# The block norms' reciprocal root in eight VectorE operations, and the weights' subtractions kept out of it

## The chip, the cores and the metric

One core of a Trainium2 chip runs the whole program in one launch. Its engines are TensorE (PE; PEld is its weight load), VectorE (DVE), ScalarE (ACT), GpSimd (POOL) and SyncE (SP), which here issues the transfers. The metric is the device time of one execution in microseconds, the median over runs.

## The reference, cut to what matters

Two blocks of depth 2 are chained over one sequence of S = 256 tokens of width D = 1024, in fp32, with FFNs of width 2816. The first block has per layer an FFN, a mixer (a gated delta net and a latent attention) and a second FFN. The second block begins with an FFN on the tokens `x` and on a context `ctx`, has a state-space mixer, two FFNs, a pool mixer and an FFN. A final norm ends it. Each of these parts is of one shape:

```python
h = x * rsqrt(mean(x * x, -1) + EPS)      # the block norm
h = h * (1 + scale) + shift               # scale, shift, gate: from the conditioning, by ada_w
x = x + gate * part(h)
```

## The kernel before, in words

The tokens lie in two tiles of 128 partitions (NT = 2), each in two halves of 512 columns. Every product with a weight is done in three matmuls with rounded parts of both operands: a weight's hi and lo part and the tokens' hi and lo part. L351 multiplies the tokens' lo with the weight's hi, L352 hi with hi, and L353 the tokens' hi with the weight's lo; only L353 needs the weight's lo.

A weight comes in units of 128x1024. `load_unit` issues the load into one of six raw buffers on SP's queue, rounds it to hi on ScalarE (L345, or L339 in halves of 512) and subtracts hi from it on VectorE (L346, or L340) to get lo. hi and lo have five buffers of their own; units loaded far ahead ("deep") use general pages `pg` and the half-size lines. Three lanes keep the order of the units: `in_order("dma" | "hi" | "lo", ins)` ties each instruction to the one that `last[kind]` holds, an order on one engine that is fixed when the program is built. All else on an engine is ordered by the scheduler, at build time too, by the program's order among what it takes to be ready.

A norm is made by `Prep`. `Prep.a(t)` squares the two halves of token tile t on ScalarE with a sum (L683), adds the two sums (L684), calls `rsqrt` (L214 to L229: L218 scales and adds EPS, L219 and L220 make the first guess out of the bits, then three steps of L223 and L227) and multiplies both halves (`scaled`, L690). The ten operations from L684 to the last L227 work on one element per partition and each needs the one before. `Prep.b(t)` then transposes on TensorE (L248), modulates while evicting (L702 on VectorE, L700 on ScalarE) and splits the result into hi (L723) and lo (L724), in `hTa` or `hTb`, which the next product reads. The pool mixer's `PoolPrep` replaces `scaled` by a product with a second tensor, `sc` (L1927), and has no `b`; its product L1947 reads the scaled rows.

At the end of a part, `ending.done(t)` multiplies with the gate (L784), adds to the stream (L785) and calls `a(t)` of the next part's norm at once, `b(t)` some units later. There, at a seam, the last eight units of a part hold the second token tile's matmuls back; while TensorE does those, the first eight units of the next part are loaded and split, and tile 0's norm is made. The context's norms, `p0` and `p1`, are made in the middle of an FFN's down-projection: `a(0)` after its fourth unit and `a(1)` after its fifth; `p1` reads its rows back out of DRAM, where the context's first FFN wrote them (L2040 writes, L2025 reads).

There are 14 such norms of two token tiles each. The very first is made while `m.first` is set (the conditioning of the first part is still being computed).

Of the kernel before, what the change touches and what calls it, by code (L numbers as in the profile page):

```python
# [12 lines left out]
I32 = mybir.dt.int32  # L13
AF = mybir.ActivationFunctionType
ALU = mybir.AluOpType
# [4 lines left out]
D = 1024  # L20
# [4 lines left out]
EPS = 1e-6  # L25
# [50 lines left out]
def block_kernel(ctx, tc, A, out):  # L76
    nc = tc.nc
    V, G, T = nc.vector, nc.gpsimd, nc.tensor
# [27 lines left out]
    def nm(s):  # L106
        names[0] += 1
        return f"{s}_{names[0]}"
# [7 lines left out]
    def pg(dt=F32):  # L116
        return pgp.tile([P, 512], dt, tag="pg", name=nm("pg"))

    def small(n, dt=F32, tag="sm", bufs=None):
        return smp.tile([P, n], dt, tag=f"{tag}{n}", name=nm(tag), **({"bufs": bufs} if bufs else {}))  # L120
# [8 lines left out]
    def C(n):  # L129
        a, w = CI[n]  # L130
        return con[:, a:a + w]
# [7 lines left out]
    def rows_load(srcs):  # L139

        st = pg()
        at = 0
        for a in srcs:
            load(st[at:at + a.shape[0], 0:P], a)
            at += a.shape[0]
        return st, at
# [28 lines left out]
    def vectors():  # L175

        if adab:
            return
        st = pg()
        at = 0  # L180
        for a in (r128(A["c"][0]), r128(A["c_2"][0]), r128(A["c_ctx_2"]), rr(A["norm_ffn1"]), rr(A["norm_mix"]),
                  rr(A["norm_ffn2"]), A["norm_g_2"].rearrange("l n (k p) -> (l n k) p", p=P)):
            load(st[at:at + a.shape[0], 0:P], a)
            at += a.shape[0]
            yield
        l_vecs = st, at
        l_first = l_adab(*first_key)
        yield
        vecs = rows_put("vecs", l_vecs)
        for b in (0, 1, 2):  # L190
            if b != first_key[0]:
                ACT.activation(cond[:, 8 * b:8 * b + 8], vecs[:, 8 * b:8 * b + 8], AF.Silu)
        gain.update({(0, l, s): vecs[:, 24 + 16 * s + 8 * l: 32 + 16 * s + 8 * l] for l in range(2) for s in range(3)})
        gain.update({(1, l, s): vecs[:, 72 + 24 * l + 8 * s: 80 + 24 * l + 8 * s] for l in range(2) for s in range(3)})
        adab[first_key] = rows_put("adab0", l_first)
# [12 lines left out]
    def bcm(ap, n):  # L208

        return ap.unsqueeze(1).to_broadcast([P, n, ap.shape[1]])  # L210
# [3 lines left out]
    def rsqrt(out_, in_, scale, eps, n):  # L214

        v, y, t = small(n, tag="rx"), small(n, tag="ry"), small(n, tag="rt")
        i = small(n, I32, tag="ri")
        V.tensor_scalar(out=v, in0=in_, scalar1=-0.5 * scale, scalar2=-0.5 * eps, op0=ALU.mult, op1=ALU.add)  # L218
        V.tensor_scalar(out=i, in0=v.bitcast(I32), scalar1=1, scalar2=None, op0=ALU.logical_shift_right)  # L219
        V.tensor_scalar(out=y.bitcast(I32), in0=i, scalar1=-1, scalar2=0x5F3759DF - 0x400000 + 0x40000000, op0=ALU.mult, op1=ALU.add)  # L220
        for k in range(3):
            if n == 1:
                V.scalar_tensor_tensor(out=t, in0=y, scalar=v, in1=y, op0=ALU.mult, op1=ALU.mult)  # L223
            else:
                V.tensor_mul(t, y, y)
                V.tensor_mul(t, t, v)
            V.scalar_tensor_tensor(out=(out_ if k == 2 else y), in0=t, scalar=1.5, in1=y, op0=ALU.add, op1=ALU.mult)  # L227
# [73 lines left out]
    last = {}  # L301
# [366 lines left out]
    class Prep:  # L668
# [9 lines left out]
        def a(self, t):  # L678
            ss, r = small(2, tag="ss"), small(1, tag="rstd")
            xh = [self.xs(t, h) for h in range(2)]  # L680
            for h in range(2):
                xn = self.xn[t, h] = pg()
                ACT.activation(xn, xh[h], AF.Square, accum_out=ss[:, h:h + 1])  # L683
            V.tensor_add(ss[:, 0:1], ss[:, 0:1], ss[:, 1:2])  # L684
            rsqrt(r, ss[:, 0:1], 1.0 / D, EPS, 1)
            for h in range(2):
                self.scaled(t, h, xh[h], r)

        def scaled(self, t, h, src, r):
            V.tensor_scalar(out=self.xn[t, h], in0=src, scalar1=r, scalar2=None, op0=ALU.mult)  # L690

        def feat(self, t, h):
            q = ps()
# [1202 lines left out]
    class PoolPrep(Prep):  # L1896
        def early(self):

            for _ in range(4):
                yield  # L1900
            self.q, self.w = [], []
            self.sums, self.bias = pg(), pg()
            for h in range(2):
                load(self.sums[32 * h:32 * h + 1, :].rearrange("p (g l) -> p g l", l=S), A["poolc"][2 * h:2 * h + 2, :].unsqueeze(0))
                load(self.bias[32 * h:32 * h + 1, :], A["pool_b_2"][0, 2 * h:2 * h + 2, :].rearrange("g d -> (g d)").unsqueeze(0))
            for g in range(4):
                self.w.append(pg())
                load(self.w[g].rearrange("p (k d) -> p k d", k=2), A["pool_w_2"][0, g].rearrange("(k p) d -> p k d", p=P))
            yield
            for h in range(2):  # L1910
                psc = pg()
                load(psc, A["pool_scale_2"][0, h * 512:(h + 1) * 512].partition_broadcast(P))
                yield
                V.tensor_mul(psc, psc, self.m.has("gate", 0)[:, h * 512:(h + 1) * 512])
                V.tensor_mul(self.bias[32 * h:32 * h + 1, :], self.bias[32 * h:32 * h + 1, :], psc[32 * h:32 * h + 1, :])
                yield
                for g in (2 * h, 2 * h + 1):
                    w_ = self.w[g].rearrange("p (k d) -> p k d", k=2)
                    V.tensor_mul(w_, w_, bcm(psc[:, g % 2 * S:g % 2 * S + S], 2))
                    yield  # L1920
            for g in range(4):
                self.q.append(pg())
                load(self.q[g].rearrange("p (t l) -> p t l", t=NT), A["poolq"][g].rearrange("(t p) l -> p t l", p=P))
            yield
# [249 lines left out]
```

## Time and profile before

| | us |
|---|---|
| median of 3 runs | 3010.07 |
| least and most of the 3 | 3007.27 and 3012.36 |
| the profiled execution, its own time | 3013.99 |
| its span in the trace | 3012.2 |
| TensorE busy | 2908.4 (97%) |
| VectorE busy | 2190.8 (73%) |
| ScalarE busy | 1356.9 (45%) |

The trace is that of one execution. Its mean granted clock of TensorE is 0.984 of full speed. Busy time counts the instructions of an engine, not its waits. In a timeline row, the brackets at the end tell how long the engine stood idle before the instruction, and what released it.

### The profile page before, as it was taken

Reading aid. Unit: us, or ns where it says so; the run is one execution under the profiler, and the core shown is the slowest. Engines: PE = TensorE matmul, PEld = TensorE weight load, DVE = VectorE, ACT = ScalarE, POOL = GpSimd, SP = SyncE. Lnnn points to the kernel's source line nnn. Section 1 sums busy time; section 2 is a strip of 40 time slices with the busy share of each in tenths; the row PEclk is TensorE's granted clock in tenths of the full one; section 3 lists DMA queues with packets and bytes.
Section 4 is the critical chain, followed back from the end, with each engine's and each line's share of the span. In section 5 each row is a group of like instructions: output and inputs, shape, how many; then the busy total and the mean of one; then the engine's idle time right before and its main releaser. Section 6 shows DMA issues by size and latency. Waiting matters only on the chain.

```text
span 3012.2 us, 42589 instructions
## 1 busy us (share of the span) xinstructions
PE 2908.4 (97%) x16059; PEld 2432.2 (81%) x16059; DVE 2190.8 (73%) x4002; ACT 1356.9 (45%) x2123; POOL 105.5 (4%) x100
## 2 busy tenths in 40 slices
PE   7999999999999999999999999999899999999998
PEld 4988776779889788767798888888776798897797
DVE  6778757777687875677987664786788875887654
ACT  4555323554454443245546222455546544543443
POOL 1000110000000002000000000000022000000000
PEclk9999999999999999999999999999999999999999
DMA  8875534468778842244676455764434586788464
GB/s 269 293 271 190 175 103 117 130 191 265 254 242 275 298 138 79 72 137 152 219 242 212 153 175 160 263 216 140 158 98 133 189 278 242 228 289 297 155 188 133
DMA packets 275496, 589.04 MB, mean 196 GB/s; under 512 B 28731, under 2 KB 72905, under 8 KB 275291
## 3 DMA queue, kind: packets, MB, share of 16 engines
q1 hardware_dynamic: 275291, 586.32, 59.6%
q8 instruction: 126, 2.06, 0.3%
q14 instruction: 79, 0.65, 0.1%
HBM read 582.05 MB, written 4.19 MB: 195 GB/s over the span
## 4 chain that ended last, share of the span: by engine, by line
PE 72%; DVE 16%; DMA 6%; ACT 3%; issue 3%; SPq 0%; DVEq 0%; ACTq 0%
PE mm L351 18%; PE mm L352 17%; PE mm L353 17%; PE mm L411 5%; PE mm L384 4%; DVE lo L346 3%; DMA ad<-ada_w 3%; PE ps L248 3%; DVE acc L540 2%; PE ps L1260 1%; ACT hi L345 1%; PE ps L1267 1%; PE ps L558 1%; DMA raw<-ffn_w_down 1%; DVE pg L1611 1%
## 5 line engine op out<-in xcount | busy, mean ns | idle before, releaser
L345 ACT CAST hi<-raw 128x1024 fp32r<-128x1024 f32 x587 | 613.9, 1048 | 876.5 <-PE mm L352 349.7
L346 DVE TENSOR_TENSOR lo<-raw,hi 128x1024 fp32r<-128x1024 f32 x587 | 710.9, 1219 | 304.9 <-ACT hi L345 295.1
L351 PE MATMUL mm<-hTa,lo 128*128 128x256 f32 (+1 forms) x2160 | 650.8, 302 | 17.6 <-DVE lo L346 9.6
L352 PE MATMUL mm<-hTa,hi 128*128 128x256 f32 (+1 forms) x2160 | 643.7, 298 | 0.0
L353 PE MATMUL mm<-hTa,hi 128*128 128x256 f32 x1872 | 531.6, 284 | 0.0
L351 PEld LDWEIGHTS mm<-hTa,lo 128*128 128x128 f32 x2160 | 414.1, 192 | 34.4 <-DVE lo L346 10.5
L352 PEld LDWEIGHTS mm<-hTa,hi 128*128 128x128 f32 x2160 | 414.4, 192 | 13.4 <-issue 1.4
L540 DVE SCALAR_TENSOR_TENSOR acc<-ad,cond,acc 128x1024 f32<-128x1024 f32 x238 | 308.3, 1295 | 88.8 <-DMA ad<-ada_w 86.6
L353 PEld LDWEIGHTS mm<-hTa,hi 128*128 128x128 f32 x1872 | 360.1, 192 | 0.0
L351 PE MATMUL mm<-hi,pg 128*128 128x512 f32 x828 | 329.5, 398 | 1.6 <-DVE pg L844 0.9
L353 PE MATMUL mm<-lo,pg 128*128 128x512 f32 x828 | 324.1, 392 | 2.7 <-DVE lo L346 2.5
L352 PE MATMUL mm<-hi,pg 128*128 128x512 f32 x828 | 323.6, 391 | 0.0
L351 PE MATMUL mm<-hi,hTa 128*128 128x512 f32 (+1 forms) x444 | 182.8, 412 | 23.0 <-DVE hTa L724 11.7
L411 PE MATMUL mm<-hTb,raw 128*128 128x256 f32 x896 | 205.0, 382 | 0.0
L411 PEld LDWEIGHTS mm<-hTb,raw 128*128 128x128 f32 x896 | 169.0, 191 | 29.5 <-issue 7.9
L351 PEld LDWEIGHTS mm<-hi,pg 128*128 128x128 f32 x828 | 156.0, 188 | 36.2 <-issue 2.2
L353 PEld LDWEIGHTS mm<-lo,pg 128*128 128x128 f32 x828 | 155.7, 188 | 36.4 <-DVE lo L346 4.2
L353 PE MATMUL mm<-lo,hTa 128*128 128x512 f32 (+1 forms) x468 | 184.1, 394 | 0.0
L352 PE MATMUL mm<-hi,hTa 128*128 128x512 f32 (+1 forms) x468 | 183.9, 393 | 0.0
L352 PEld LDWEIGHTS mm<-hi,pg 128*128 128x128 f32 x828 | 156.0, 188 | 32.9 <-issue 2.2
L384 PE MATMUL mm<-raw,hTb 128*128 128x512 f32 x320 | 151.0, 603 | 0.0
L340 DVE TENSOR_TENSOR pg<-raw,pg 128x512 fp32r<-128x512 f32 x202 | 128.8, 683 | 4.9 <-ACT pg L339 3.4
(461 smaller groups left out, 4407.7 us busy)
## 6 DMA issues: line engine op xcount, KB each, us to landing
ad<-ada_w SPq DMA_DIRECT2D x272, 512.0 KB
raw<-ffn_w SPq DMA_DIRECT2D x264, 512.0 KB
raw<-ffn_w_down SPq DMA_DIRECT2D x110, 512.0 KB
raw<-w_in SPq DMA_DIRECT2D x104, 512.0 KB
raw<-ffn_w_gate SPq DMA_DIRECT2D x88, 512.0 KB
raw<-ffn_w_up SPq DMA_DIRECT2D x88, 512.0 KB
raw<-ssd_w_in SPq DMA_DIRECT2D x60, 512.0 KB
raw<-w_branch_a SPq DMA_DIRECT2D x16, 512.0 KB
```

Source lines behind the costliest of these rows:

```text
L248: T.transpose(o[:, sl], src[:, sl], ident)
L340: in_order(lane, eng.tensor_sub(lo[j], r, hi[j]))
L345: in_order("hi", ACT.copy(hi[:, 0:m], raw[:, 0:m]))
L346: in_order(lane, eng.tensor_sub(lo[:, 0:m], raw[:, 0:m], hi[:, 0:m]))
L351: T.matmul(o, sl, mh, start=first, stop=False)
L352: T.matmul(o, sh, mh, start=False, stop=False)
L353: T.matmul(o, sh, ml, start=False, stop=last)
L384: T.matmul(d[c0 // 512][:, 0:min(cw, c0 + 512) - c0], sf, wt[c0 // 512], start=k == 0, stop=k == kt - 1)
L411: T.matmul(acc[m][:, 0:S], wt[0][:, SL[m]], hT.whole[:, k, :], start=k == 0, stop=k == KD - 1)
L540: after_edge(V.scalar_tensor_tensor(out=o, in0=w, scalar=sc, in1=o, op0=ALU.mult, op1=ALU.add))
L558: T.matmul(q, ones, self.acc[i][h], start=True, stop=True)
L1260: T.matmul(blk(y[:, H2[h]]), M[t][:, sl], odd(Ub[t][:, sl]), start=True, stop=True)
```

## The change

`Prep.a` no longer adds the two sums and calls `rsqrt`. One operation with a pointer scalar makes s = ss0 + ss1 + D·EPS; one integer operation makes the first guess out of the bits of s, with the opposite sign and off by a constant factor; three steps of two operations each follow. What the steps leave out, the factor -sqrt(2D), goes into `scaled` as a second multiplication in the same instruction, and for the pool mixer into its tensor `sc`, by one more operation for each half in `early`. These are eight chained operations on one element per partition in place of ten. The last of them is put into `last["lo"]`, other than in the first norm: every weight's subtraction that comes later in the program must stand behind it on VectorE. The norm itself is not tied to the subtractions before it.

```diff
--- before.py
+++ after.py
@@ -681,13 +681,21 @@
             for h in range(2):
                 xn = self.xn[t, h] = pg()
                 ACT.activation(xn, xh[h], AF.Square, accum_out=ss[:, h:h + 1])
-            V.tensor_add(ss[:, 0:1], ss[:, 0:1], ss[:, 1:2])
-            rsqrt(r, ss[:, 0:1], 1.0 / D, EPS, 1)
+
+            s, z, u = small(1, tag="rx"), small(1, tag="ry"), small(1, tag="rt")
+            V.tensor_scalar(out=s, in0=ss[:, 0:1], scalar1=ss[:, 1:2], scalar2=D * EPS, op0=ALU.add, op1=ALU.add)
+            V.tensor_scalar(out=z.bitcast(I32), in0=s.bitcast(I32), scalar1=-0.5, scalar2=0x5F3759DF - 0x400000, op0=ALU.mult, op1=ALU.add)
+            for k in range(3):
+                V.scalar_tensor_tensor(out=u, in0=z, scalar=s, in1=z, op0=ALU.mult, op1=ALU.mult)
+                ins = V.scalar_tensor_tensor(out=(r if k == 2 else z), in0=u, scalar=-1.5, in1=z, op0=ALU.add, op1=ALU.mult)
+
+            if last.get("lo") is not None and self.m.first is None:
+                last["lo"] = ins.ins
             for h in range(2):
                 self.scaled(t, h, xh[h], r)
 
         def scaled(self, t, h, src, r):
-            V.tensor_scalar(out=self.xn[t, h], in0=src, scalar1=r, scalar2=None, op0=ALU.mult)
+            V.tensor_scalar(out=self.xn[t, h], in0=src, scalar1=r, scalar2=-(2.0 * D) ** 0.5, op0=ALU.mult, op1=ALU.mult)
 
         def feat(self, t, h):
             q = ps()
@@ -1912,6 +1920,7 @@
                 load(psc, A["pool_scale_2"][0, h * 512:(h + 1) * 512].partition_broadcast(P))
                 yield
                 V.tensor_mul(psc, psc, self.m.has("gate", 0)[:, h * 512:(h + 1) * 512])
+                V.tensor_scalar(out=self.m.has("sc", 0)[h], in0=self.m.has("sc", 0)[h], scalar1=-(2.0 * D) ** 0.5, scalar2=None, op0=ALU.mult)
                 V.tensor_mul(self.bias[32 * h:32 * h + 1, :], self.bias[32 * h:32 * h + 1, :], psc[32 * h:32 * h + 1, :])
                 yield
                 for g in (2 * h, 2 * h + 1):
```

## Rows read from the trace of the kernel before

**Rows 1.** Profile page: busy time by engine, shares of the last chain

```profile
PE 2908.4 (97%) x16059; PEld 2432.2 (81%) x16059; DVE 2190.8 (73%) x4002; ACT 1356.9 (45%) x2123; POOL 105.5 (4%) x100
PE 72%; DVE 16%; DMA 6%; ACT 3%; issue 3%; SPq 0%; DVEq 0%; ACTq 0%
```

**Rows 2.** Waits of TensorE: line, waited for, us in total, times, longest us

```profile
PE mm L351 <- DVE hTa L724: 11.7, 9, 3.3
PE mm L351 <- DVE lo L346: 9.6, 7, 5.2
PE ps L1729 <- ACT pg L1616: 6.6, 1, 6.6
PE ps L248 <- DVE pg L690: 2.4, 6, 1.2
PE ps L1947 <- DVE pg L1927: 1.9, 1, 1.9
```

**Rows 3.** Timeline of VectorE, an undisturbed norm: start us, us, operation

```profile
2785.53 0.15 DVE L684 TENSOR_TENSOR ss<-ss 128x1 f32<-128x1 f32 x1
...
2785.72 0.15 DVE L218 TENSOR_SCALAR rx<-ss 128x1 f32<-128x1 f32 x1
...
2786.28 0.22 DVE L223 SCALAR_TENSOR_TENSOR rt<-ry,rx 128x1 f32<-128x1 f32 x1
2786.54 0.16 DVE L227 SCALAR_TENSOR_TENSOR ry<-rt,ry 128x1 f32<-128x1 f32 x1
2786.73 0.22 DVE L223 SCALAR_TENSOR_TENSOR rt<-ry,rx 128x1 f32<-128x1 f32 x1
...
2787.63 1.41 DVE L1927 SCALAR_TENSOR_TENSOR pg<-xres,rstd,pg 128x512 f32<-128x512 f32 x2
```

**Rows 4.** Timeline of VectorE, seam from the FFN to layer 1's mixer

```profile
1039.30 0.14 DVE L684 TENSOR_TENSOR ss<-ss 128x1 f32<-128x1 f32 x1
1039.47 0.69 DVE L340 TENSOR_TENSOR pg<-raw,pg 128x512 fp32r<-128x512 f32 x1
...
1042.87 0.68 DVE L340 TENSOR_TENSOR pg<-raw,pg 128x512 fp32r<-128x512 f32 x1
...
1046.87 0.87 DVE L690 TENSOR_SCALAR pg<-xres,rstd 128x512 f32<-128x512 f32 x2
```

**Rows 5.** That seam on TensorE; window: engines' busy us, clock, DMA share

```profile
1047.49 1.06 PE L248 MATMUL ps<-con,pg 128*128 128x128 f32 x8 [1.15 <-DVE pg L690]
1051.89 0.36 PE L351 MATMUL mm<-hi,hTa 128*128 128x208 f32 x1 [3.33 <-DVE hTa L724]
...
1051.90:1056.20 4.30, 4.30 (x24) 4.30 (x25) 3.02 (x13) 0.81 (x2) 0.00 (x0) 0.60 0.07 22
```

**Rows 6.** Instructions by tile: count, least/median/most ns, first and last start, forms

```profile
L690 DVE TENSOR_SCALAR pg<-xres,rstd x44: 474/483/1007, 8.9 to 2812.0; 128x512 f32<-128x512 f32 x44
L1927 DVE SCALAR_TENSOR_TENSOR pg<-xres,rstd,pg x4: 744/748/752, 2784.2 to 2788.3; 128x512 f32<-128x512 f32 x4
```

**Rows 7.** Timelines of VectorE and TensorE around the pool mixer

```profile
2778.19 0.15 DVE L684 TENSOR_TENSOR ss<-ss 128x1 f32<-128x1 f32 x1
...
2784.20 1.41 DVE L1927 SCALAR_TENSOR_TENSOR pg<-xres,rstd,pg 128x512 f32<-128x512 f32 x2
...
2811.11 0.77 PE L351 MATMUL mm<-hi,hTa 128*128 128x512 f32 x1 [3.73 <-DVE rstd L227]
```

**Rows 8.** VectorE, ScalarE and a window at the context norms of layer 1

```profile
1966.12 4.62 DVE L346 TENSOR_TENSOR lo<-raw,hi 128x1024 fp32r<-128x1024 f32 x4
...
1970.01 0.63 ACT L683 ACTIVATE pg<-pg 128x512 f32<-128x512 f32 x1 [1.04 <-DMA pg<-xctx]
...
1972.05 0.16 DVE L684 TENSOR_TENSOR ss<-ss 128x1 f32<-128x1 f32 x1 [1.30 <-ACT pg L683]
...
1975.21 0.63 ACT L683 ACTIVATE pg<-pg 128x512 f32<-128x512 f32 x1 [0.76 <-DMA pg<-xctx]
...
1970.00:1974.00 4.00, 4.00 (x19) 3.34 (x18) 2.56 (x9) 3.44 (x7) 0.00 (x0) 1.00 0.93 340
```

## Prediction

> **What bounds the kernel now.** I read the page's busy line and chain first: PE is busy 2908.4 of 3012.2 us and makes up 72% of the chain that ended last, DVE 16% [rows 1]. So DVE, 73% busy, costs time only where PE stands still for it, and 103.8 us (3012.2 − 2908.4) is all that PE stands still. Of that, the view of PE's waits shows what a norm can touch: 11.7 us in 9 waits for the hTa that L724 writes from normed rows, 2.4 us in 6 for L690's scaled rows, 1.9 us in one for L1927; a further 9.6 us in 7 waits are for a weight's lo from L346, which this change delays [rows 2]. Then I read the timeline around those waits: the norm's chain alone [rows 3], with weights' subtractions inside it [rows 4], PE behind it [rows 5], the pool mixer [rows 7] and the context norms [rows 8]. The reader is to see there that the same ten tiny operations take 2.10 us when nothing stands between them and 7.57 us when subtractions do.
>
> **The shorter chain.** An undisturbed norm runs from L684 at 2785.53 to the scaling L1927 at 2787.63: 2.10 us for ten dependent operations [rows 3]. From start to start an operation with immediates takes 0.19 us (2785.53 to 2785.72), one with a pointer scalar 0.26 (L223, 2786.28 to 2786.54), and the immediate one behind it 0.19 (L227, to 2786.73). L218 has two immediate operations and the same 0.15 us as L684, so operations inside an instruction are free. The new chain is one with a pointer (0.26), one plain (0.19) and three pairs (0.26 + 0.19 each, 1.35): 1.80 us, 0.30 less. Over the block norms, 14 of two token tiles, that is 28 x 0.30 = 8.4 us of DVE time, most of it beside a busy PE, and only a wait of PE turns it into time. The factor that `scaled` gets rides as a second immediate operation: between nothing (as L218 shows) and 0.26 us for each 128x512 (L1927's 748 ns with two tensors against L690's 483 [rows 6]); I take nothing. The two multiplications added to the pool's `early`, near 0.48 us each by L690, fall among FFN matmuls, under a busy PE: nothing; without that cover 1.0 us.
>
> **The pin at the worst seam (FFN to mixer, layer 1).** Between L684 at 1039.30 and L690 at 1046.87 lie 7.57 us, with six L340 (the first at 1039.47, the last at 1042.87) and two L346 inside [rows 4]. All come later in the program than this norm, so all must now stand behind it, and L690 could start near 1039.30 + 1.80 = 1041.1. PE's transposes start at 1047.49 after 1.15 us of waiting for L690, so the other token tile's matmuls end near 1046.3; and the mixer's first product at 1051.89 after 3.33 us of waiting for L724. Then the granted clock is 0.60 over 4.30 us, 1.7 us lost [rows 5]. Small bound: the transposes just start on time, −1.15. Large bound: they and their evictions move up among the other tile's matmuls, and both waits and the slow stretch go: 1.15 + 3.33 + 1.7 = 6.2. But the eight subtractions, some 6.4 us, are still to be done by DVE, now between L690 and the evictions, so I take the middle, **−3.5** (−6.2 to −1.2).
>
> **The other seams and the SSD norms.** The other eight waits for L724 sum to 8.4 us (11.7 − 3.3), the other five for L690 to 1.2 (2.4 − 1.2) [rows 2]. The shorter chain gives 13 × 0.30 = 3.9 there. More would be had where subtractions stand inside, but each of them is done right after the norm, where DVE also has the evictions and PE then waits for a lo instead: the 7 waits for L346, one of 5.2 us, lie in such stretches. Bounds −9.6 and +3 (a third of those 9.6 us again); I take **−3.5**. L1729's one wait of 6.6 us for ScalarE's L1616 [rows 2] follows the SSD mixer's norms; what they give there is inside this term.
>
> **The pool mixer.** L684 at 2778.19 to L1927 at 2784.20 is 6.01 us, with two L346 and the other tile's four L784 and L785 inside; PE waits 1.92 us for it. With the subtractions out, the chain's 1.80 us and those four put it ahead of PE's need: −1.9. But the first weights of the FFN behind the pool may now be subtracted only behind the next norm, for whose rstd PE has waited until 2811.11 [rows 7]; there it starts on that weight, and two lo's of 1.2 us would then still be ahead: +1 (0 to +2.5). Together **−0.9** (−1.9 to +2.5).
>
> **The context norms: the loss.** Norms `p0` and `p1` run in the middle of an FFN's down-projection, under a busy PE, where nobody waits for them; weights' subtractions do not wait for them either. With the pin they do. At `p1` four L346 run from 1966.12 to 1970.74 while the norm's squares wait for a DMA out of DRAM: 1970.01 on ACT, L684 only at 1972.05; the second tile's first square is at 1975.21 [rows 8]. After the change those of the four whose unit follows the norm in the program (from the fifth unit on) stand behind the norm: 1972.05 + 1.80, and 1.15 for the subtraction itself: 1975.0. PE is busy all of 1970 to 1974 with 19 matmuls, 0.21 us each; at 12 a unit it takes a unit in some 2.6 us, and counted unit by unit along its timeline it wants this lo near 1971.1: 3.9 us late. Only L353 reads a weight's lo, so up to 8 matmuls, 1.8 us, can be put ahead. Behind that, the unit after the second norm waits for two squares of some 0.7 us from 1975.21, to 1976.6, so its lo comes near 1979.5 against a need at 1973.8, or 1977 if everything has already slipped or its loads come sooner. Queued behind the held subtraction are all later subtractions on DVE (the pin and the lane keep them in order), and by raw buffers that are not freed the weights' loads on SP's queue, with them the context's own reads. Ends: +2 (3.9 less 1.8) and +7.4 (5.7, and 1.7 of slow clock as behind the 3.33 us wait [rows 5]); I take **+4**. At `p0` the rows come from an input that nothing delays, and the lo is about in time: **+0.5** (0 to +4).
>
> By the Trainium skill, "TensorE: Matmul & The Clock Gate", section "Why this matters for your kernels", idle gaps between bursts of matmuls bring the engine's clock down, which would speak against a change that opens a new gap at the context norms. The trace agrees in kind (0.60 behind the wait of 3.33 us).
>
> The Trainium skill, "VectorE: DVE Perf Modes", section "The TRN2 errata", puts 58 cycles at 0.96 GHz and the elements on an instruction, which is an estimate of 0.06 us for a one-element operation; by that two operations fewer would give 0.12 us a norm and the sum would be near −1. The rows' 0.15 to 0.22 us decide.
>
> **Sum.** −3.5 − 3.5 − 0.9 + 4 + 0.5 = −3.4 us. The profiled execution took 3013.99, so 3010.6 by its own time; it lies 3.9 above the median of 3010.07, to which I apply the same difference: **3007 us**.
>
> **Rivals.** What a measurement of this kernel can tell from no change is 0.2%, 6 us: below 3004 is faster, above 3016 slower.
> A, the likeliest: seams gain about 8, the context norms give half of it back; 3007, own range 3004 to 3016.
> B, faster: the context norms do not stall. The order on every engine is laid out anew at build time; if the context's reads and squares go out one unit (2.6 us) sooner, or PE has enough other products, the +4.5 falls away, and with the transposes moved up at the seam (−2.7 more) the sum is −10.6: 2999. If half the other seams' waits go as well, 2995. For it: those waits are visible, and PE gains from nothing else. Against: ACT's row at 1970.01 waits 1.04 us for the read itself.
> C, slower: one mechanism, the weights' lane held behind the context norms. If the held lo's also hold back raw buffers and so the reads of the second tile, `p1` costs 10 (7.4 and one unit of 2.6), `p0` 4, and the gains shrink to 4 because DVE is full behind the seams: +10, 3020. It decides from a stall of 10 us with gains of 4, or of 14 with all 7.9. For it: PE's full stretch at 1970 to 1974 has no slack. Against: the 1.8 us of other products in each unit bridge much.
> D: the order changes only off PE's path; no change, 3010, inside A.
>
> **Chances.** A with D 0.46, B 0.34, C 0.20: faster 0.34, same 0.46, slower 0.20. The range that leaves out no more than 2 in 10 runs from B's far end to just short of C: 2995 to 3019.
>
> **What would show it.** Right: L690 or L1927 some 1.8 us behind the last square in every norm, no L340 or L346 inside; the waits at the seam under 2 us in place of 1.15 and 3.33; at `p1` a new wait of PE for L346 of 2 to 6 us. Wrong: that wait is absent (B), or there are two or more of over 4 us (C); or the seam's product still waits 3 us for L724 because the eight subtractions stand ahead of the evictions; or the time moves in places without a norm, by a new order alone.

## The result and the profile after

The changed kernel takes 3026.79 us (median of 8 runs, 3018.08 to 3031.42) where the kernel before takes 3009.76 (8 runs, 3005.65 to 3012.88). The ratio is 1.0056, with an interval of 1.0043 to 1.007: 13 to 21 us slower. The profiled execution took 3026.84 us, its span is 3025.0.

The page after answers to [rows 1]: busy time of each engine, then the chain's shares.

```profile
PE 2908.3 (96%) x16059; PEld 2422.9 (80%) x16059; DVE 2186.0 (72%) x3948; ACT 1356.2 (45%) x2123; POOL 103.8 (3%) x100
PE 67%; DVE 18%; DMA 7%; ACT 4%; issue 3%; SPq 0%; DVEq 0%; ACTq 0%
```

TensorE works as long as before, 2908.3 us against 2908.4, and VectorE 4.8 us less. By the busy count the 12.8 us that the span grew are TensorE's idle time, though busy time can hide slower products, as the pool mixer will show. VectorE's share of the chain grew by two points. The waits of TensorE answer to [rows 2] (line, what it waited for, us in total, times, longest):

```profile
PE mm L351 <- DVE hTa L732: 10.6, 10, 2.5
PE mm L351 <- DVE lo L346: 10.8, 7, 5.2
PE mm L353 <- DVE lo L346: 8.0, 6, 2.5
PE mm L353 <- DVE pg L340: 3.8, 5, 1.7
PE ps L248 <- DVE pg L698: 2.0, 3, 0.9
```

L724 is L732 now, L690 is L698, L1946 and L1947 are L1955 and L1956. The waits for normed rows hardly fell: 11.7 us became 10.6, 2.4 became 2.0. New are waits of L353 for a weight's lo: 3.8 us for L340, which the view of before does not have, and 8.0 us for L346, of which before shows 2.5. (L353 reads the weight's lo in the products of `tok_units`, and so in all the stretches below. In those of `feat_units` the operands of L351 and L353 change places, and it is L351 that reads it: L351's waits for L346, 9.6 us before and 10.8 after, are waits for a weight's lo too.)

**The norm itself** did what was forecast. This is VectorE's timeline, the pool mixer's first norm; it answers to [rows 3] and [rows 7].

```profile
2780.72 0.21 DVE L686 TENSOR_SCALAR rx<-ss 128x1 f32<-128x1 f32 x1 [0.86 <-ACT pg L683]
2780.97 0.15 DVE L687 TENSOR_SCALAR ry<-rx 128x1 int32<-128x1 int32 x1
...
2782.50 1.41 DVE L1936 SCALAR_TENSOR_TENSOR pg<-xres,rstd,pg 128x512 f32<-128x512 f32 x2
```

Eight operations, nothing between them: 1.78 us from L686 to L1936, and 0.25 us behind the one with the pointer scalar.

**Where the time went.** Both kernels run the same number of matmuls, 16059, so the start of the n-th matmul can be set against the start of the n-th in the other trace. That gives how much longer each stretch became. The stretches are named by the times of before; the figures are us more than before, each from one profiled execution.

| stretch of before | what lies in it | after | chain_only | no_pin_ctx | no_pin_pool | sums_first | alternate_before | pin_one |
|---|---|---|---|---|---|---|---|---|
| 225 to 330 | FFN to layer 0's mixer | +3.3 | +0.3 | +1.4 | +1.4 | +1.3 | +0.6 | +0.2 |
| 822 to 875 | FFN to FFN | +1.4 | -0.6 | +1.4 | +1.4 | +1.4 | 0.0 | -0.6 |
| 925 to 985 | inside an FFN | -5.2 | -4.4 | -2.3 | -3.5 | -3.9 | -4.7 | -4.1 |
| 1025 to 1080 | FFN to layer 1's mixer | -2.2 | +0.2 | -5.4 | +0.1 | -4.1 | +0.2 | -2.6 |
| 1160 to 1215 | inside the mixer | -2.3 | 0.0 | -1.7 | -1.7 | -1.7 | -1.7 | -2.0 |
| 1580 to 1615 | context norms p0 | +0.4 | 0.0 | 0.0 | +0.4 | +0.4 | 0.0 | 0.0 |
| 1950 to 2010 | context norms p1 | +6.9 | -0.5 | +0.5 | +7.1 | +5.4 | +0.3 | +1.7 |
| 2560 to 2640 | FFN to FFN | +1.1 | +0.1 | +1.2 | +1.0 | +0.7 | -0.3 | -0.2 |
| 2765 to 2810 | pool mixer | +5.1 | -0.4 | +3.5 | -0.7 | -3.1 | +13.1 | -0.9 |
| 2810 to 2850 | FFN behind it | +5.0 | +0.3 | +7.8 | +0.9 | +6.2 | -0.3 | +0.7 |

The columns beside "after" are the experiments below. The reader is to see three places that cost: p1, the pool mixer and the FFN behind it, 17.0 us together, and one that gains. The gains at 925 and at 1160 also stand in the column of a kernel that changes nothing there (alternate_before, −4.7 and −1.7); the profiled execution of before took longer in these stretches. It took 3013.99 us against a median of 3009.76.

**The pool mixer.** TensorE's timeline before, then after. L1946 (L1955 after) are the eight products over one row, L1947 (L1956) the sixteen over 128 rows that read the normed tile, each of them two matmuls; L1960 (L1969) ends the stretch.

```profile
2780.12 1.34 PE L1946 MATMUL ps<-pg,pg 1*128 1x256 f32 x5
...
2781.30 0.37 PE L1946 MATMUL ps<-pg,pg 1*128 1x256 f32 x1
2781.41 0.37 PE L1946 MATMUL mm<-pg,pg 1*128 1x256 f32 x1
2781.52 0.37 PE L1946 MATMUL ps<-pg,pg 1*128 1x256 f32 x1
...
2785.01 3.78 PE L1947 MATMUL ps<-pg,pg 128*128 128x256 f32 x8 [1.92 <-DVE pg L1927]
...
2790.99 1.89 PE L1947 MATMUL ps<-pg,pg 128*128 128x256 f32 x8
...
2794.53 1.12 PE L1960 MATMUL mm<-pg,con 1*128 1x512 f32 x2
```

```profile
2782.85 0.69 PE L1955 MATMUL ps<-pg,pg 1*128 1x256 f32 x2
2783.47 0.70 PE L1956 MATMUL ps<-pg,pg 128*128 128x256 f32 x2
...
2787.25 1.22 PE L1956 MATMUL ps<-pg,pg 128*128 128x256 f32 x2
2788.40 1.22 PE L1955 MATMUL mm<-pg,pg 1*128 1x256 f32 x2
...
2802.67 1.12 PE L1969 MATMUL mm<-pg,con 1*128 1x512 f32 x2
```

Before, the sixteen one-row matmuls stand first and run while TensorE has to wait for L1927 anyway; then come the others, 14.41 us in all (2780.12 to 2794.53). After, the two kinds take turns, two by two, in the order in which the program has them, and the stretch takes 19.82 us (2782.85 to 2802.67), although TensorE waits for nothing in it. A pair takes 0.62 us at first and 1.15 later. The windows tell the second step (engines' busy us, granted clock, DMA share, GB/s), first after, then before:

```profile
2783.00:2787.00 4.00, 4.00 (x14) 1.91 (x14) 3.31 (x6) 1.18 (x4) 0.00 (x0) 1.00 0.00 0
2787.00:2791.00 4.00, 4.00 (x9) 1.80 (x8) 2.92 (x10) 0.16 (x2) 0.00 (x0) 0.52 0.00 0
...
2783.00:2819.00 36.00, 32.59 (x97) 18.74 (x97) 16.26 (x48) 8.40 (x23) 0.00 (x0) 0.79 0.00 0
```

```profile
2782.00:2784.00 2.00, 1.08 (x7) 0.59 (x4) 1.90 (x7) 1.16 (x3) 0.00 (x0) 0.78 0.98 355
2784.00:2788.00 4.00, 2.99 (x7) 2.46 (x8) 3.61 (x14) 0.21 (x2) 0.00 (x0) 0.50 0.48 175
2788.00:2811.00 23.00, 19.38 (x74) 13.12 (x73) 11.46 (x38) 6.94 (x18) 0.00 (x0) 0.95 0.00 0
```

The granted clock is 1.00 until 2787 and 0.52 and less behind it, the lower of its two levels (1.2 and 2.4 GHz), though TensorE was busy 4.00 of 4.00 us in both windows. At the clock of 1.00 two matmuls in turn take 0.62 us, 0.31 each; before, full ones in a row are 0.22 apart (eight from 2790.99 to 2792.72) and so are one-row matmuls into ps (2781.30 and 2781.52), while those into mm, whose rows lie on another partition, run beside them (2781.41). The Trainium skill, "TensorEngine Tiling (Array Packing)", section "Tiling Modes", says that a change of tiling mode drains the engine; the 0.31 us agrees with that, but no run here shows in which mode a one-row matmul runs.

**Behind the pool mixer.** VectorE's, TensorE's and SP's timelines after:

```profile
2818.77 1.22 DVE L346 TENSOR_TENSOR lo<-raw,hi 128x1024 fp32r<-128x1024 f32 x1
```

```profile
2834.63 0.50 PE L353 MATMUL mm<-pg,hTa 128*128 128x512 f32 x1 [1.74 <-DVE pg L340]
```

```profile
2775.90 1.57 SPq L325 DMA_DIRECT2D raw<-ffn_w_up  x2
...
2820.05 4.93 SPq L325 DMA_DIRECT2D raw<-ffn_w_up  x2
```

The first weight of the FFN behind the pool has its lo subtracted at 2818.77, behind the last operation of that FFN's norm (2818.70). Before, three L346 stood at 2777 to 2780, just ahead of the pool mixer's norm and inside it; they freed raw buffers, and loads ran in 2782 to 2788 (shares 0.98 and 0.48 above). After, SP issues no weight's load between 2777.5 and 2820.05, and the DMA engines move nothing in the 36 us from 2783 to 2819 (0.00). Most of such a gap was there before: from 2788 to 2811 they moved nothing either (0.00). What the pin takes away is the loads of 2782 to 2788, some 1.4 MB by the rates in the windows. The weights come late by that, and L353 waits for L340, at 2834.63 for 1.74 us.

**The context norms p1.** VectorE, TensorE and two windows; they answer to [rows 8].

```profile
1967.95 0.21 DVE L686 TENSOR_SCALAR rx<-ss 128x1 f32<-128x1 f32 x1 [4.70 <-ACT pg L683]
...
1970.10 1.22 DVE L346 TENSOR_TENSOR lo<-raw,hi 128x1024 fp32r<-128x1024 f32 x1
...
1976.49 1.22 DVE L346 TENSOR_TENSOR lo<-raw,hi 128x1024 fp32r<-128x1024 f32 x1
```

```profile
1971.37 0.74 PE L353 MATMUL mm<-lo,pg 128*128 128x512 f32 x2 [1.42 <-DVE lo L346]
...
1977.77 0.88 PE L353 MATMUL mm<-lo,pg 128*128 128x512 f32 x2 [2.46 <-DVE lo L346]
```

```profile
1974.00:1978.00 4.00, 1.54 (x11) 1.17 (x10) 3.99 (x12) 2.88 (x7) 0.00 (x0) 1.00 0.01 2
1978.00:1982.00 4.00, 4.00 (x12) 3.12 (x12) 4.00 (x6) 0.79 (x1) 0.00 (x0) 0.57 0.73 174
```

VectorE, which before did four subtractions here, stands still 4.70 us until the square is there, and its next L346 comes at 1970.10, behind the norm, the one after the second norm at 1976.49. TensorE waits 1.42 and 2.46 us, the granted clock is 0.57 in the four us behind, and the DMA share falls to 0.01, while no L346 frees a raw buffer (none runs between those of 1970.10 and 1976.49).

**The seam that gains.** VectorE, TensorE and a window at layer 1's mixer answer to [rows 4, 5]:

```profile
1036.73 0.16 DVE L690 SCALAR_TENSOR_TENSOR rstd<-rt,ry 128x1 f32<-128x1 f32 x1
1036.81 1.02 DVE L346 TENSOR_TENSOR lo<-raw,hi 128x832 fp32r<-128x832 f32 x1
1037.74 0.88 DVE L698 TENSOR_SCALAR pg<-xres,rstd 128x512 f32<-128x512 f32 x2
```

```profile
1045.78 0.36 PE L351 MATMUL mm<-hi,hTa 128*128 128x208 f32 x1 [0.65 <-DVE hTa L732]
1053.74 1.06 PE L248 MATMUL ps<-con,pg 128*128 128x128 f32 x8 [0.87 <-DVE pg L698]
1058.65 0.36 PE L351 MATMUL mm<-hi,hTa 128*128 128x208 f32 x1 [2.46 <-DVE hTa L732]
```

```profile
1045.00:1049.00 4.00, 3.35 (x27) 3.18 (x27) 3.91 (x8) 3.26 (x6) 0.00 (x0) 1.00 0.87 266
```

No transpose of token tile 0 waits, the first product waits 0.65 us in place of 1.15 and 3.33, and the clock stays at 1.00. Tile 1 waits 0.87 us for L698 and 2.46 for L732, where it waited 1.92 and 0.80 us for L724 before.

### The profile page after: what moved, and what is told of

Same layout as the page of the kernel before. It is cut to its first block, busy times and chain, and to the rows that moved or that the text cites. A ratio compares the mean times of both kernels' runs of the same rounds, so it can differ in the third digit from the quotient of the medians.

```text
span 3025.0 us, 42533 instructions
## 1 busy us (share of the span) xinstructions
PE 2908.3 (96%) x16059; PEld 2422.9 (80%) x16059; DVE 2186.0 (72%) x3948; ACT 1356.2 (45%) x2123; POOL 103.8 (3%) x100
## 4 chain that ended last, share of the span: by engine, by line
PE 67%; DVE 18%; DMA 7%; ACT 4%; issue 3%; SPq 0%; DVEq 0%; ACTq 0%
PE mm L351 16%; PE mm L353 16%; PE mm L352 16%; PE mm L411 5%; PE mm L384 4%; DMA ad<-ada_w 4%; DVE lo L346 4%; PE ps L248 2%; DVE acc L540 2%; PE ps L1268 1%; ACT hi L345 1%; DVE pg L340 1%; PE ps L1275 1%; PE ps L558 1%; DMA raw<-ffn_w_down 1%
## 5 line engine op out<-in xcount | busy, mean ns | idle before, releaser
L346 DVE TENSOR_TENSOR lo<-raw,hi 128x1024 fp32r<-128x1024 f32 x587 | 709.8, 1219 | 296.6 <-ACT hi L345 287.8
L351 PE MATMUL mm<-hTa,lo 128*128 128x256 f32 (+1 forms) x2160 | 649.7, 301 | 14.8 <-DVE lo L346 10.8
L353 PE MATMUL mm<-hTa,hi 128*128 128x256 f32 x1872 | 530.5, 284 | 0.0
L351 PEld LDWEIGHTS mm<-hTa,lo 128*128 128x128 f32 x2160 | 413.0, 191 | 31.4 <-DVE lo L346 11.7
L353 PEld LDWEIGHTS mm<-hTa,hi 128*128 128x128 f32 x1872 | 359.1, 192 | 0.0
L351 PE MATMUL mm<-hi,pg 128*128 128x512 f32 x828 | 329.8, 398 | 1.9 <-DVE pg L2047 0.8
L353 PE MATMUL mm<-lo,pg 128*128 128x512 f32 x828 | 323.7, 392 | 8.1 <-DVE lo L346 8.0
L351 PE MATMUL mm<-hi,hTa 128*128 128x512 f32 (+1 forms) x444 | 181.6, 409 | 21.8 <-DVE hTa L732 10.6
L353 PEld LDWEIGHTS mm<-lo,pg 128*128 128x128 f32 x828 | 155.8, 188 | 43.0 <-DVE lo L346 10.9
L351 PEld LDWEIGHTS mm<-hi,pg 128*128 128x128 f32 x828 | 155.9, 188 | 36.9 <-issue 2.2
L353 PE MATMUL mm<-lo,hTa 128*128 128x512 f32 (+1 forms) x468 | 183.3, 393 | 0.1
L340 DVE TENSOR_TENSOR pg<-raw,pg 128x512 fp32r<-128x512 f32 x202 | 128.4, 683 | 5.0 <-ACT pg L339 3.3
```

Of the source, the lines that this page charges most:

```text
L340: in_order(lane, eng.tensor_sub(lo[j], r, hi[j]))
L346: in_order(lane, eng.tensor_sub(lo[:, 0:m], raw[:, 0:m], hi[:, 0:m]))
L351: T.matmul(o, sl, mh, start=first, stop=False)
L353: T.matmul(o, sh, ml, start=False, stop=last)
```

## The experiments

Ratios are to the kernel before, timed on the same chip beside each, with their 95% intervals.

**chain_only**: the eight operations without the pin.

```diff
-            if last.get("lo") is not None and self.m.first is None:
-                last["lo"] = ins.ins
```

> The change without the pin: eight operations, and no weight's subtraction tied to a norm. Theory 1 (the pin costs at the pool mixer and at the context norms, and the shorter chain by itself is harmless): as before or up to 4 us faster, 3006 to 3010, with no wait of L353 for L340 behind the pool mixer and the one-row matmuls of the pool all ahead of the others, as before. Rival (the new chain itself, or the order that any change of it makes, costs the time): 8 us or more over before.

3007.59 us, ratio 0.9988 (0.9977 to 0.9999): by the ratio 3.6 us faster. The waits at p1 are gone, the one-row products stand first, and the wait of 3.37 us at layer 1's mixer is there as before. Behind the pool L353 still waits for L340 twice, 0.43 and 0.63 us, where none was expected; the stretch there is 0.3 us longer than before. The new chain is no part of the loss.

**pin_only**: the old ten operations with the pin.

```diff
...
-            rsqrt(r, ss[:, 0:1], 1.0 / D, EPS, 1)
+            ins = rsqrt(r, ss[:, 0:1], 1.0 / D, EPS, 1)
+            if last.get("lo") is not None and self.m.first is None:
+                last["lo"] = ins.ins
```

> The kernel before with the pin alone: the old ten operations, the last of them put in front of every later subtraction. Theory 1 (the whole loss is the pin's, the shorter chain gives at most 4 us): 17 to 22 us over before. Rival (the new chain has a part in the loss): 12 us over before or less.

3029.21 us, ratio 1.0053 (1.0034 to 1.0072), 16 us over before: a little under what was expected, within its interval as much as the whole change. The pin is the loss. Its places are not quite the same: p1 costs 7.4 us, the FFN behind the pool 5.3, layer 0's mixer 4.0, but the pool mixer's stretch is 2.1 us shorter than before. With the longer chain four of the eight one-row products still stand first there, ahead of any other, and the stretch from the first of them takes 12.31 us (2783.91 to 2796.22). So the full turns need both parts of the change.

**no_pin_ctx**: the pin taken from p0 and p1. A norm now has a mark `pin`; the condition on it stands in the next experiments too, and is not printed again.

```diff
+        pin = True
...
-            if last.get("lo") is not None and self.m.first is None:
+            if last.get("lo") is not None and self.m.first is None and self.pin:
...
+    p0.pin = p1.pin = False
```

> The changed kernel with the pin taken from the context's norms p0 and p1 alone. Theory 1: 5 to 8 us less than the changed kernel (about 3020), the waits of L353 for L346 of 1.42 and 2.46 us and the slow clock behind them gone; still some 10 us over before, all of it at the pool mixer. Rival (the context norms are the whole loss, as rival C of the prediction had it): 14 us or more less, back to before or under it.

3021.03 us, ratio 1.0038 (1.0024 to 1.0051): 5.4 us less than the changed kernel by the two ratios (0.18%). Their intervals overlap, so the times alone do not settle this much; the trace does: the stretch of p1 is 0.5 us longer than before in place of 6.9. The rival, by which this was the whole loss, falls.

**no_pin_pool**: the pin taken from the pool mixer's norm and from that of the FFN behind it.

```diff
...
     class PoolPrep(Prep):
+        pin = False
...
     def pool_mix(prep, m, nxt):
+        nxt.pin = False
```

> The changed kernel with the pin taken from the pool mixer's norm and from the norm of the FFN behind it. Theory 1: 9 to 12 us less than the changed kernel (about 3016): the one-row matmuls stand ahead of the others again, and no L353 waits for L340 behind the pool. Rival (the loss is spread over all seams or made at the context norms): 4 us less at most.

3017.84 us, ratio 1.0023 (1.001 to 1.0036): 9.9 us less than the changed kernel. The one-row products stand first again, and the two stretches are −0.7 and +0.9 us. Two waits of L353 for L340 stay behind the pool, of 0.44 and 0.75 us, where none was expected; chain_only has the like without any pin.

**no_pin_behind_pool**: the second of these two alone, so that the pool mixer's own norm keeps the pin.

```diff
...
     def pool_mix(prep, m, nxt):
+        nxt.pin = False
```

> The changed kernel with the pin taken from one norm alone, that of the FFN behind the pool mixer; the pool mixer's own norm keeps it. Theory 1: the turns of the one-row products stay (the pool's stretch 5 us longer than before), the waits of L353 for L340 behind it go (the 39 us from 2811 on as long as before, in place of 5 to 8 us longer): 5 to 8 us less than the changed kernel. Rival (the late subtractions there come from the pool mixer's own pin, which moved three of them back): under 2 us less, the waits for L340 stay.

3019.27 us, ratio 1.0033 (1.0022 to 1.0043): 7 us less than the changed kernel. The pool mixer's stretch is 5.1 us longer than before, as with the full change, and the one behind it 0.4 us shorter (two waits of 0.47 and 0.90 us for L340 stay). The late loads are made by the norm behind the pool, the turns by the pool's own: two L346 are done right behind the pool's norms, at 2780.87 and 2783.33, and the loads that they let go run early again (a window, DMA share 0.76):

```profile
2783.00:2787.00 4.00, 4.00 (x9) 1.65 (x7) 1.54 (x2) 0.00 (x0) 0.00 (x0) 0.50 0.76 203
```

**sums_first**: the changed kernel with the one-row products written first.

```diff
-                if t == 0:
-                    T.matmul(o, row(sh[k // 4], k // 4)[:, SL[k % 4]], row(prep.sums, k // 4)[:, g % 2 * S:g % 2 * S + S], start=True, stop=False)
...
+        for k in range(8):
+            T.matmul(qs[k // 2][k % 2][:, 0:S], row(sh[k // 4], k // 4)[:, SL[k % 4]], row(prep.sums, k // 4)[:, k // 2 % 2 * S:k // 2 % 2 * S + S], start=True, stop=False)
         for t in range(NT):
             for g in range(4):
                 pool(g, t)
```

> The changed kernel, pins and all, with the pool mixer's eight one-row products written ahead of its other products in the program, so that they no longer take turns with them on TensorE. Theory 1: 4 to 6 us less than the changed kernel; the stretch from the first of these products to the last is as long as before (about 14.4 us in place of 19.8), while the waits for L340 behind the pool stay. Rival (the stretch is longer because of the clock that falls in any case, not because of the turns): under 2 us less.

3018.82 us, ratio 1.0029 (1.0017 to 1.0041): 8 us less than the changed kernel, more than expected. TensorE's timeline there:

```profile
2783.29 1.34 PE L1957 MATMUL ps<-pg,pg 1*128 1x256 f32 x5
...
2786.23 2.72 PE L1954 MATMUL ps<-pg,pg 128*128 128x256 f32 x8
...
2791.48 1.89 PE L1954 MATMUL ps<-pg,pg 128*128 128x256 f32 x8
...
2795.03 1.12 PE L1970 MATMUL mm<-pg,con 1*128 1x512 f32 x2
```

The stretch takes 11.74 us (2783.29 to 2795.03), 2.7 less than before: with the pin, the pool's norm is early enough that TensorE no longer waits for it. That is what the forecast had counted on (−1.9). The waits behind the pool stay, 6.2 us more than before.

The same stretch in windows, of the changed kernel, of this one and of pin_only, where half the one-row products take turns:

```profile
2782.85:2802.67 19.82, 19.82 (x49) 10.92 (x49) 7.65 (x19) 2.78 (x8) 0.00 (x0) 0.66 0.00 1
2783.29:2795.03 11.74, 11.74 (x50) 9.40 (x49) 7.66 (x19) 2.78 (x8) 0.00 (x0) 0.85 0.00 1
2783.91:2796.22 12.31, 12.31 (x50) 8.24 (x49) 7.97 (x22) 2.78 (x8) 0.00 (x0) 1.00 0.00 1
```

TensorE is busy throughout in all three, so length times granted clock estimates what each would take at the full clock: 13.1, 10.0 and 12.3 us. Of the 8.1 us between the changed kernel and this one, some 3 are the turns themselves and some 5 the lower clock. In the four traces with complete turns the clock over this stretch is 0.57 to 0.72, in those with the one-row products first 0.75 to 0.87; but in pin_only it does not fall. That complete turns go with a longer stretch at the lower clock is shown, that they cause it is not.

**alternate_before**: the kernel before, its one-row products made to take turns.

```diff
...
-                    T.matmul(o, row(sh[k // 4], k // 4)[:, SL[k % 4]], row(prep.sums, k // 4)[:, g % 2 * S:g % 2 * S + S], start=True, stop=False)
+                    one = T.matmul(o, row(sh[k // 4], k // 4)[:, SL[k % 4]], row(prep.sums, k // 4)[:, g % 2 * S:g % 2 * S + S], start=True, stop=False)
+                    if k:
+                        tc.add_manual_dep(one.ins, full[0].name, NOSYNC, reason="in turn")
-                T.matmul(o, u[t, k // 4][:, SL[k % 4]], prep.q[g][:, t * S:t * S + S], start=False, stop=t == NT - 1)
+                full[0] = T.matmul(o, u[t, k // 4][:, SL[k % 4]], prep.q[g][:, t * S:t * S + S], start=False, stop=t == NT - 1).ins
```

> The kernel before with only the order of the pool mixer's products changed: each one-row product L1946 is tied behind the full product of the pair before it, so that the two kinds take turns on TensorE as they do in the changed kernel; nothing is pinned. Theory 1 (the turns themselves are slow): 3 to 6 us over before, the stretch of these 24 products 3 us longer or more. Rival (the products are slow in the changed kernel for another reason, such as the clock alone): within 2 us of before.

3022.87 us, ratio 1.004 (1.0027 to 1.0054): 12 us over before, twice what was expected at most. TensorE's timeline, and a window:

```profile
2770.92 0.69 PE L1947 MATMUL ps<-pg,pg 1*128 1x256 f32 x2
2775.79 1.22 PE L1950 MATMUL ps<-pg,pg 128*128 128x256 f32 x2 [4.18 <-DVE pg L1927]
2776.94 1.22 PE L1947 MATMUL ps<-pg,pg 1*128 1x256 f32 x2
...
2798.43 1.12 PE L1963 MATMUL mm<-pg,con 1*128 1x512 f32 x2
```

```profile
2775.00:2793.00 18.00, 17.21 (x31) 7.93 (x32) 4.47 (x14) 0.00 (x0) 0.00 (x0) 0.50 0.09 34
```

The stretch takes 27.51 us (2770.92 to 2798.43). Here the wait for L1927 is 4.18 us, since 14 of the 16 one-row matmuls now stand behind it, and the turns run at a clock of 0.50 from their start, 1.15 us a pair. The order of these 24 products alone, with no pin and the old chain, is worth 12 us, the longer wait (4.18 us against 1.92) and the lower clock included; the expectation had left out that the turns also uncover the wait.

**no_pin_ctx_pool**: both exceptions together.

```diff
...
+    p0.pin = p1.pin = False
...
     class PoolPrep(Prep):
+        pin = False
...
     def pool_mix(prep, m, nxt):
+        nxt.pin = False
```

> The changed kernel with the pin taken from the context's norms and from the two norms around the pool mixer, and left on all the others. Theory 1 (the two losses are separate and add): 15 to 17 us less than the changed kernel, within 4 us of before, with both stretches as long as before. Rival (a loss moves on to the next place when one is mended): still 6 us or more over before.

3008.47 us, ratio 0.9995 (0.9982 to 1.0009): 18 us less than the changed kernel, and as fast as before. The losses add (5.4 and 9.9 singly, 15 in all, each a difference of two ratios with some 4 us of interval) and do not move on. But it is not faster than chain_only: what the other pins give at layer 1's mixer (1.5 us in its trace) they take at two FFN seams and at layer 0's mixer (1.4, 1.1 and 1.4).

**pin_one**: the new chain everywhere, the pin on layer 1's mixer norm alone.

```diff
+        pin = False
...
+    preps[keys.index((0, 1, 1))].pin = True
```

> The changed kernel with the pin on one norm alone, that of layer 1's mixer, whose seam showed waits of 1.15 and 3.33 us before and 0.65 us after. Theory 1: 2 to 6 us under the kernel with the new chain and no pin, so 5 to 9 us under before, the one version that beats both. Rival (what the first token tile gains there, the second gives back): within 2 us of the kernel with the new chain and no pin, 2 to 5 us under before.

3003.2 us (12 runs), ratio 0.9972 (0.9959 to 0.9985): 8 us under before. It beats the kernel before and the changed one. Under chain_only it is by 5 us by the two ratios, but their intervals overlap, and of the two profiled executions chain_only's is the shorter (3002.61 us against 3005.22): that this one pin gains anything over none is not shown by the times. TensorE's waits at the seam, the first of them:

```profile
1042.75 0.36 PE L351 MATMUL mm<-hi,hTa 128*128 128x208 f32 x1 [0.65 <-DVE hTa L732]
```

They are near those of the changed kernel, 0.65 us, then 0.85 for L698 and 2.46 for L732: the gain of tile 0 with part of it given back at tile 1.

## Why the prediction was wrong

The prediction said 3007 us, 2995 to 3019. The measured median lies 17 us above it, on the side of rival C, for a reason that C had only in part. By its own steps (the figures of the table, against the terms):

- **The shorter chain**: right. 1.78 us against 1.80 forecast, and the second multiplication in `scaled` costs nothing (two L698 in 0.88 us, two L690 in 0.87 in [rows 4]). By itself it is worth 3.6 us (chain_only, with an interval of 0.3 to 7), near the 3.9 of the step.
- **The worst seam**, −3.5 (−6.2 to −1.2): −2.2 in the changed kernel, −5.4 to +0.1 in the other kernels with the pin there. The mechanism was right, and the transposes did move up (none of them waits). The step left out tile 1, for which TensorE now waits 0.87, 2.46 and 0.72 us, 4.1 in all, against 1.92 and 0.80 before.
- **The other seams**, −3.5 (−9.6 to +3): wrong in sign. Layer 0's mixer costs 3.3 us (4.0 in pin_only, 1.3 to 1.5 in the other kernels with the pin there), two FFN seams 1.4 and 1.1, both with a new wait of 1.13 us for L732. The subtractions that leave the norm land before the evictions. These three seams make 5.8 us, beyond the +3 that the step had as its bound; some 1.7 of them are the clock at layer 0's mixer (0.66 over 257 to 262, where no_pin_pool has 1.00 over 255 to 262).
- **The context norms**, +4 (+2 to +7.4) and +0.5: right in place and kind, +6.9 and +0.4. Two waits, 1.42 and 2.46 us, the slow clock and the loads that stop are what was forecast; they come near the upper end.
- **The pool mixer**, −0.9 (−1.9 to +2.5): the step that failed, +10.0 us. Two things were not in it. It took the order of TensorE's products as given; but the scheduler lays it out by what it takes to be ready, and a norm that is ready earlier lets the full products in between the one-row products, with turns and a lower clock: a stretch 5.4 us longer where −1.9 was forecast (shown by sums_first and alternate_before). And it counted two late subtractions of 1.2 us behind the pool, not the raw buffers that they hold: the loads of 2782 to 2788 are missing, and 5 to 8 us are lost when the weights are needed (shown by no_pin_behind_pool).

The terms as measured, −2.2 + 3.3 + 1.4 + 1.1 + 6.9 + 0.4 + 10.0, make some +21. The spans differ by 12.8, since the trace of before took longer in stretches that the change does not touch, and the medians by 17.

Rival C named the right mechanism, the weights' lane held behind norms that wait for something else, but placed it at p0 and p1 alone. Its sign came out; at its own place the price was 6.9 us where it said 10, and without the pool it would have made the kernel slower by no more than about 0.2%: no_pin_pool is at 1.0023.

What stays open: why the clock fell at layer 0's mixer in this trace and in pin_only alone, and whether pin_one gains over chain_only at all, though its seam is 2.8 us shorter. One profiled execution of each does not tell that from its scatter.

## What to carry to other kernels

A pin that keeps work out of a short chain also ties that work to whatever the chain waits for; put it only where the trace shows that the chain is what the bound engine waits for, here at most one part's norm of fourteen, and not where the chain waits for a transfer or stands ahead of a refill. When something is made ready earlier, ask what the scheduler will move into the gap on the bound engine, and read its new order before the sum. A held instruction's price is not its own length but that of the buffers it holds: compare the DMA share behind it with the one before the change.

## What the runs showed of the hardware

TensorE's granted clock fell from 1.00 to 0.52 while the engine was busy 4.00 of 4.00 us, when one-row and full matmuls of 256 columns took turns (2783 to 2791 after). In sums_first it also fell (0.57 in 2787 to 2791), behind sixteen one-row matmuls in a row, in windows in which TensorE was again busy 4.00 of 4.00 us. In both the lower level follows one-row matmuls without a wait of TensorE. It does not follow them each time: in pin_only, with eight in a row and eight in turn, the clock stayed at 1.00 over the 12.31 us. And matmuls of two shapes in turn cost 0.31 us each at the full clock, against 0.22 when a kind stands in a row; one-row matmuls whose rows lie on two partitions came 0.11 apart, and the sixteen of before were done in 3.0 us (2780.12 to 2783.09).
